# Tracing the last transposes of each half ahead of two block products in the MLP input of a decoder layer

## The chip, the cores and the metric

The kernel runs on one core of one Trainium2 chip. The metric is the device time of one execution in microseconds (us); the median of three runs of the kernel before is 2172.05 us (2169.45 to 2173.22).

## The reference

One decoder layer on a sequence of 2048 tokens of width 1024, in float32. The first part, a mixer of dilated attention and a gated recurrence, is not touched by the change. What matters here is the second part, the MLP, with its norms:

```python
def rms_norm(x, g):
    y = xf * lax.rsqrt(jnp.mean(xf * xf, axis=-1, keepdims=True) + NORM_EPS)
    return (y * g).astype(x.dtype)

def squared_relu_mlp(h, w1, w2):
    a = jax.nn.relu(h @ w1)
    return (a * a) @ w2

x = x + rms_norm(m, mix_norm_post[l])          # m: the mixer's output, (2048, 1024)
h = rms_norm(x, mlp_norm_pre[l])
x = x + rms_norm(squared_relu_mlp(h, w_ff_in[l], w_ff_out[l]), mlp_norm_post[l])
```

`w_ff_in` (w1) is 1024 x 4096, `w_ff_out` (w2) 4096 x 1024.

## The kernel before

**Precision.** Each float32 factor of a product is split in a high and a low part (`split`, L54): ScalarE (ACT) casts the high part (L56, rows named CAST), VectorE (DVE), in some places GpSimd (POOL), subtracts it to get the low part (L57). TensorE (PE) then does three matmuls per tile, high x high, low x high and high x low.

**Halves.** After the mixer's first part the kernel works through two halves of 1024 tokens (`half`, L2129, with hf = 0 and 1). Each half has eight blocks of 128 tokens, t = 0 to 7. For each block PE does the mixer's output projection (`OutProj.product`, L882, tiles m). `OutProj.finish` (L901) does the norm and residual on ACT and DVE; its last two DVE instructions (L927) write the normalised input h2 of the block into the tile xt, 512 columns each. xt's place is one of five in a ring of 128 x 1024 tiles, which also takes the loads of w1 (w1r).

**Columns.** `Factors.columns(t)` (L978) turns a block's h2 round: eight 128x128 transposes on PE (L989, tiles h2t), in two groups of four, q = 1 for the right half of xt and q = 0 for the left. ACT copies the first group out (L992); DVE, in the last four blocks, subtracts the second from it (L994) and so makes T3. Both tiles h2t come from a ring of two PSUM banks, B, which the tiles zc use as well. A block's transposes are traced two blocks after its norm; those of block 6 come after the first product of the MLP, those of block 7 later still.

**The MLP's input product** h @ w1 is done by a scheme of seven block products in place of eight (Strassen's in Winograd's form). The right factors are sums of blocks of h2, each with a high (hH) and a low (hL) part: B11, B21 and T3 are made in `columns`, T2, T4, T1 and B22 in `Factors.late` (L1009), after block 7's columns. Products 1 and 2 need B11 and B21, product 7 needs T3, product 6 T2, product 5 T1, product 3 B22, product 4 T4. Each needs all 512 columns of its factor. The left factors f are sums of blocks of w1; `mlp_in` (L1068) runs over 16 pairs j of rows of w1. For pairs 0 and 1, and for products 1 and 2 of pair 2 in the second half, they were made earlier and are loaded by SyncE (SP, L1094); the others are made from loads w1r (L1086) with sums on DVE (L1115). A pair is a generator whose steps are the products 1 (into PSUM tile za), 2 (zb), 7 (zc), 6, 5, 3 (again into za) and 4 (into zc); a product is 12 matmuls of 128x512 (L1104 to L1106). Between them ACT copies za to the tile sq (L1143 after product 1, L1148 after product 6, L1152 after 5), and only behind that copy may PE add the next product to za. Outputs are squared on ACT (L1109, L1110) and summed (L1113, L1167).

**What sets the order.** The code only traces instructions. A planner (`Plan`, L1496, with the simulation `Machine`, L1693) then gives each engine an order: it takes PE's instructions in about the order in which they were traced, as due times (`clock`), works back from them to the time at which each other instruction is needed (`need`), and simulates the engines, each taking the ready instruction that is needed first. An instruction on PE that isn't ready can be passed by a later one. The engines then keep to the order that comes out. So moving a step in the trace moves due times, and can move instructions on all engines.

The steps around the change, in `half`, with `pairs` the generators of the pairs:

```python
pairs = mlp_in(tc, sh, scr, hf, F.H, w1, w2, place)
next(pairs[0])                                   # pair 0: product 1
columns(NQH - 2)                                 # transposes of block 6
for j in (0, 1, 1, 2):                           # 0: product 2; 1: products 1, 2; 2: product 1
    next(pairs[j])
columns(NQH - 1)                                 # transposes of block 7
for j in (2, 0):                                 # 2: product 2; 0: product 7
    next(pairs[j])
```

Of the kernel before, what the change touches and what calls it, by code (L numbers as in the profile page):

```python
# [853 lines left out]
def mix_columns(nc, sh, scr, hf, order, t):  # L854

    mx = {}
    for g0 in range(0, KT, 4):
        n = f"{hf}_{t}_{g0}"
        hi, lo = sh.pair(f"m{n}", (P, 4, P))
        k0 = order[g0]  # L860
        sh.mixed = nc.sync.dma_start(out=f32(lo), in_=scr["mix"][hf][k0:k0 + 4, :, t * P:(t + 1) * P].rearrange("k p t -> p k t"))
        split_there(nc, hi, lo, nc.vector if hf and t == 0 else nc.gpsimd)
        for i, k in enumerate(order[g0:g0 + 4]):
            mx[k] = (hi[:, i, :], lo[:, i, :])
    return mx
# [321 lines left out]
def mlp_in_rest(pairs):  # L1187

    for j in range(0, NJ, 2):
        both = pairs[j:j + 2]  # L1190
        for i in TURNS[min(j // 2, 2)]:
            next(both[i])
        if j == NJ - 2:
            yield
        for x in both:
            next(x)
# [792 lines left out]
def trunk(tc, x, xT, g1, g2, g3, g4, w_in, w_v, conv_w, conv_b, w_r, b_r, w_i, b_i, lam, w_out, w1, w2,  # L1989
# [4 lines left out]
    def sb(name, side):  # L1994
        return tc.tile_pool(name=name, bufs=1, side=side, reuse_waits="tile")
# [5 lines left out]
    with (  # L2001
# [127 lines left out]
        def half(hf, wo, mx):  # L2129

            with contextlib.ExitStack() as st:
                F = Factors(nc, sh, hf, st.enter_context(sb(f"hA{hf}", "left")))
                h2 = {}
                po = st.enter_context(sb(f"op{hf}", "left"))
                with contextlib.nullcontext():

                    place = [po.tile([P, 4, TB], F32, name=f"place{hf}")]
                    op = OutProj(tc, sh, po, scr, hf, wo, order, x, g2, g3, sh.mixed if hf else None)

                    def columns(t):  # L2140
                        F.columns(cst["ident"], t, h2.pop(t))

                    for t in range(NQH):
                        m = [op.product(t, 0, mx[t])]
                        if t > 1:
                            columns(t - 2)
                        m.append(op.product(t, 1, mx[t]))
                        h2[t] = op.finish(t, m)
                        if t < NQH - 2:
                            with tc.issue_after(op.squared.ins):  # L2150
                                mx.append(mix_columns(nc, sh, scr, hf, order, t + 2))
                    wst.close()
                    F.tiles(st.enter_context(sb(f"hB{hf}", "right")), F.LATE)
                    pairs = mlp_in(tc, sh, scr, hf, F.H, w1, w2, place)
                    next(pairs[0])
                    columns(NQH - 2)
                    for j in (0, 1, 1, 2):
                        next(pairs[j])
                    columns(NQH - 1)
                    for j in (2, 0):  # L2160
                        next(pairs[j])
                    made = F.done
                    for step in (1, "T2", 0, "T4", 1, "T1", 0, 1, "B22"):
                        with tc.issue_after(made[0].ins), tc.issue_after(made[1].ins):
                            if step in F.LATE:
                                made = F.late(step)
                            else:
                                next(pairs[step])
                sh.made = made[1]
                end = mlp_in_rest(pairs)  # L2170
                next(end)
            return end
# [4 lines left out]

        with per, tc.manual_schedule(engines={mybir.EngineType.PE}):
            end = half(0, wo, ready)
            with sb("y0", "left") as pl, sb("z0", "left") as p:  # L2180
                rest = mlp_out(tc, sh, p, cst, scr, 0, w2, g4, out, pl)
# [19 lines left out]
                with tc.issue_after(cst["load"].ins):  # L2201
                    ready = [mix_columns(nc, sh, scr, 1, order, t) for t in range(2)]
            end = half(1, wo, ready)
            with sb("y1", "left") as pl, sb("z1", "left") as p:
                rest = mlp_out(tc, sh, p, cst, scr, 1, w2, g4, out, pl)
# [69 lines left out]
```

## Time and profile before

| | |
|---|---|
| median of three runs | 2172.05 us |
| the profiled execution's own time | 2171.24 us |
| its span, first to last instruction | 2169.4 us |
| mean granted clock of TensorE | 0.995 |
| busy: TensorE / VectorE / ScalarE / GpSimd | 98% / 70% / 58% / 22% |
| transposes of block 7, first and second half | at 707.66 and 1560.92 us |

The profile's rows name a line, an engine, an operation, the tile written, an arrow, the tiles read, their shapes and a count. In rows in order of time the first number is the start in us from the span's start, the second the duration; a bracket at the end tells how long the engine was idle just before, and what it waited for. Matmuls overlap: one starts about 0.23 us after the one ahead of it, and each lasts about 0.39. Rows of waits read "who <- for whom: us in total, times, longest". In the table by stretches the granted clock is given as a share of full speed, and the DMA share is the mean busy share of the core's 16 DMA engines.

### The profile page before, as it was taken

How to read it: one execution, taken by the hardware profiler on the slowest of the kernel's cores; microseconds unless marked ns; L12 is line 12 of the kernel's file. 1: busy time of each engine (PE TensorE's matmuls, PEld its weight loads, DVE VectorE, ACT ScalarE, POOL GpSimd, SP SyncE). 2: the span in 40 equal slices, each digit the busy share in tenths (PEclk: the TensorE clock that was granted, in tenths of full speed). 3: DMA queues.
4: the chain of work that ended last, by engine and by line, in shares of the span. 5: the costliest groups of instructions: out<-in, count | busy, mean ns of one | idle time of the engine just before them, and what ended most of it. 6: DMA issues, size and time to landing. Idle time of an engine off the chain costs nothing.

```text
span 2169.4 us, 30821 instructions
## 1 busy us (share of the span) xinstructions
PE 2129.0 (98%) x10232; PEld 1752.5 (81%) x10232; DVE 1510.2 (70%) x2883; ACT 1255.2 (58%) x2516; POOL 483.2 (22%) x552
## 2 busy tenths in 40 slices
PE   8999999999999999999999999999999999999998
PEld 6777878777788788888888888888788888888887
DVE  4468777768877777775776868787765665665556
ACT  6458666646554655554766667764465555654442
POOL 2454443477622001000011101113100000000003
PEclk9999999999999999999999999999999999999999
DMA  9555556456965667779787785796634444866665
GB/s 346 163 182 163 174 170 203 158 167 238 325 211 190 242 251 297 281 271 354 240 229 221 234 255 173 227 301 192 230 130 175 146 160 144 326 204 193 193 192 179
DMA packets 220899, 473.50 MB, mean 218 GB/s; under 512 B 23412, under 2 KB 74388, under 8 KB 214468
## 3 DMA queue, kind: packets, MB, share of 16 engines
q1 hardware_dynamic: 191924, 337.52, 48.2%
q0 software_dynamic: 28816, 134.01, 17.3%
q8 instruction: 81, 1.33, 0.3%
q14 instruction: 78, 0.64, 0.1%
HBM read 337.09 MB, written 151.13 MB: 225 GB/s over the span
## 4 chain that ended last, share of the span: by engine, by line
PE 84%; DVE 5%; ACT 5%; DMA 2%; POOL 2%; issue 2%; SPq 1%; DVEq 0%; ACTq 0%; POOLq 0%
PE o L1254 9%; PE o L1256 9%; PE o L1255 9%; PE za L1105 5%; PE za L1106 5%; PE za L1104 5%; PE z L229 4%; PE z L230 4%; PE z L231 4%; PE m L889 3%; PE m L891 3%; PE m L890 3%; PE zc L1105 3%; PE zc L1106 3%; PE zc L1104 3%; PE oB L672 2%
## 5 line engine op out<-in xcount | busy, mean ns | idle before, releaser
L229 PE MATMUL z<-hH,wH 128*128 128x512 f32 x576 | 228.8, 397 | 4.5 <-DVE zn L258 4.5
L231 PE MATMUL z<-hH,wL 128*128 128x512 f32 x576 | 228.4, 396 | 0.0
L230 PE MATMUL z<-hL,wH 128*128 128x512 f32 x576 | 228.2, 396 | 0.0
L229 PEld LDWEIGHTS z<-hH,wH 128*128 128x128 f32 x576 | 108.9, 189 | 31.1 <-DVE zn L258 5.8
L230 PEld LDWEIGHTS z<-hL,wH 128*128 128x128 f32 x576 | 108.9, 189 | 24.8 <-issue 4.5
L231 PEld LDWEIGHTS z<-hH,wL 128*128 128x128 f32 x576 | 108.8, 189 | 22.6 <-issue 2.3
L57 POOL TENSOR_TENSOR wL<-wraw,wH 128x512 fp32r<-128x512 f32 x68 | 100.6, 1491 | 101.9 <-ACT wH L56 80.8
L1169 POOL DMA_DIRECT2D sa<-sq x31 | 16.5, 532 | 375.2 <-ACT sq L1110 375.2
L1109 ACT ACTIVATE sq<-sq 128x512 f32<-128x512 f32 x93 | 58.8, 632 | 70.7 <-DVE sq L1113 70.7
L452 ACT ACTIVATE smB<-smB,stB 128x128 f32<-128x128 f32 (+3 forms) x128 | 71.5, 560 | 39.0 <-DVE stB L446 38.8
L452 ACT ACTIVATE sm<-sm,stA 128x256 f32<-128x256 f32 (+1 forms) x128 | 63.4, 497 | 50.9 <-DVE stA L446 50.7
L57 DVE TENSOR_TENSOR tlB<-pT_B,thB 128x384 fp32r<-128x384 f32 x96 | 57.2, 599 | 33.7 <-ACT thB L56 31.1
L1110 ACT ACTIVATE sq<-sq 128x512 f32<-128x512 f32 x124 | 76.9, 630 | 2.6
L446 DVE CUSTOM_DVE_ANT_0 sm<-S,mask_a 128x256 f32<-128x256 f32 (+1 forms) x128 | 47.7, 408 | 33.1 <-PE S L589 29.3
L1288 POOL TENSOR_TENSOR y<-y,g4b 128x512 f32<-128x512 f32 x8 | 12.5, 1578 | 257.1 <-ACT junk_y L86 257.1
L56 ACT CAST wH<-wraw 128x512 fp32r<-128x512 f32 x72 | 42.1, 616 | 43.5 <-PE z L230 24.5
L446 DVE CUSTOM_DVE_ANT_0 smB<-SB,mask_b 128x128 f32<-128x128 f32 (+3 forms) x128 | 59.6, 486 | 7.1 <-PE SB L647 3.6
L56 ACT CAST thB<-pT_B 128x384 fp32r<-128x384 f32 x96 | 48.9, 511 | 24.3 <-PE pT_B L425 19.6
L425 PE MATMUL pT_B<-ident,smB 128*128 128x128 f32 x320 | 59.6, 277 | 2.1 <-DVE tlA L57 1.2
L341 DVE SCALAR_TENSOR_TENSOR xc<-xr,cw,xc 128x512 f32<-128x512 f32 x48 | 48.1, 1001 | 6.7 <-POOL xc L338 6.4
L1104 PE MATMUL za<-hHT,f_6H 128*128 128x512 f32 x128 | 50.4, 395 | 1.7 <-ACT hHT L56 1.7
L1105 PE MATMUL za<-hLT,f_6H 128*128 128x512 f32 x128 | 50.7, 396 | 1.3 <-DVE hLT L57 1.3
(615 smaller groups left out, 7180.1 us busy)
## 6 DMA issues: line engine op xcount, KB each, us to landing
sa<-as POOLq DMA_DIRECT2D x31, 1024.0 KB, 6.9
w1r<-in_dram SPq DMA_DIRECT2D x56, 512.0 KB, 3.7
sa<-sq POOLq DMA_DIRECT2D x31, 768.0 KB, 3.9
wraw<-in_dram SPq DMA_DIRECT2D x72, 256.0 KB, 3.6
place<-in_dram SPq DMA_DIRECT2D x14, 1024.0 KB, 6.6
sb<-place POOLq DMA_DIRECT2D x14, 1024.0 KB, 4.3
vb<-sv SPq DMA_DIRECT2D x24, 512.0 KB, 6.1
kh<-sk SPq DMA_DIRECT2D x24, 512.0 KB, 5.5
```

The costliest lines, as they stand in the source:

```text
L57: (lo_eng or nc.vector).tensor_tensor(out=lo, in0=src, in1=f32(hi), op=ALU.subtract))
L229: pe.matmul(z, hi[:, k, :], hh, start=(k == 0), stop=False)
L230: pe.matmul(z, hi[:, k, :], hl, start=False, stop=False)
L231: pe.matmul(z, lo[:, k, :], hh, start=False, stop=(k == KT - 1))
L446: v.tensor_tensor_reduce(out=sm[:, c0:c0 + w], in0=sp[:, c0:c0 + w], in1=mask[:, mask.shape[-1] - w:], scale=1.0, scalar=3.0e38, op0=ALU.a ...
L452: s.activation(out=sm[:, c0:c0 + w], in_=sm[:, c0:c0 + w], func=AF.Exp, scale=-1.0, bias=st[:, 0, u, cols[j]:cols[j] + 1], accum_out=st[:, ...
L1104: pe.matmul(o, hi[:, k], bh[:, k], start=start and k == 0, stop=False, skip_group_check=True)
L1105: pe.matmul(o, hi[:, k], bl[:, k], start=False, stop=False, skip_group_check=True)
L1106: pe.matmul(o, lo[:, k], bh[:, k], start=False, stop=k == KH - 1, skip_group_check=True)
L1254: pe.matmul(o, ah[:, ts], bh, start=fresh and j == 0, stop=False, skip_group_check=True)
L1255: pe.matmul(o, ah[:, ts], bl, start=False, stop=False, skip_group_check=True)
L1256: pe.matmul(o, al[:, ts], bh, start=False, stop=j == NJ - 1, skip_group_check=True)
```

## The change

The transposes of block 7 are traced two steps earlier: after pair 0's product 2 and pair 1's product 1, and so ahead of pair 1's product 2 and pair 2's product 1. The order of the products among themselves is the same in the trace.

```diff
-                    next(pairs[0])
+                    for j in (0,):
+                        next(pairs[j])
                     columns(NQH - 2)
-                    for j in (0, 1, 1, 2):
+                    for j in (0, 1):
                         next(pairs[j])
                     columns(NQH - 1)
-                    for j in (2, 0):
+                    for j in (1, 2, 2, 0):
                         next(pairs[j])
```

On PE, in the first half, at the transposes of block 7. In the names hHB21 is the high part of B21, hLT1 the low part of T1; f0_1_2H is the high part of the left factor of half 0, pair 1, product 2; a last number tells tiles apart that are traced at different places.

```order
-L1106 MATMUL za0_2_7164<-hHB11_0_6248,f0_2_1L_7159 128x512
-L989 MATMUL h2t0_7_1_7177<-ident_60,xt7_6940 128x128 x4
-L989 MATMUL h2t0_7_0_7183<-ident_60,xt7_6940 128x128 x4
+L1104 MATMUL zb0_1_7157<-hHB21_0_6250,f0_1_2H_7153 128x512
+L1105 MATMUL zb0_1_7157<-hLB21_0_6251,f0_1_2H_7153 128x512
+L1106 MATMUL zb0_1_7157<-hHB21_0_6250,f0_1_2L_7154 128x512
+L1104 MATMUL zb0_1_7157<-hHB21_0_6250,f0_1_2H_7153 128x512
+L1105 MATMUL zb0_1_7157<-hLB21_0_6251,f0_1_2H_7153 128x512
+L989 MATMUL h2t0_7_1_7139<-ident_60,xt7_6940 128x128 x4
+L1106 MATMUL zb0_1_7157<-hHB21_0_6250,f0_1_2L_7154 128x512
+L989 MATMUL h2t0_7_0_7145<-ident_60,xt7_6940 128x128 x4
```

They stood behind the last matmul of pair 2's product 1. Now the first group stands behind the fifth matmul of pair 1's product 2, and the second one matmul later. In the second half all eight now stand behind the third matmul of that product.

On PE, in the first half, between the products 6 and 5 of the pairs 0 and 1:

```order
 L1106 MATMUL za0_0_7078<-hHT2_0_7066,f0_0_6L_7264 128x512
-L1104 MATMUL za0_0_7078<-hHT1_0_7070,f0_0_5H_7322 128x512
-L1105 MATMUL za0_0_7078<-hLT1_0_7071,f0_0_5H_7322 128x512
-L1106 MATMUL za0_0_7078<-hHT1_0_7070,f0_0_5L_7323 128x512
-L1104 MATMUL za0_0_7078<-hHT1_0_7070,f0_0_5H_7322 128x512
-L1105 MATMUL za0_0_7078<-hLT1_0_7071,f0_0_5H_7322 128x512
 L1104 MATMUL za0_1_7126<-hHT2_0_7066,f0_1_6H_7293 128x512
```

Five matmuls of pair 0's product 5 stood ahead of pair 1's product 6. Now they follow it, and product 5 is whole.

On DVE, in the second half, behind the subtraction that makes the last columns of T3 (L994). ws and w1r with 1_3 in their names are sums of pair 3's blocks of w1:

```order
-L994 TENSOR_TENSOR h2r1_12_14634<-h2r1_22_14637,h2t1_7_0_15573 128x4x128
-L1115 TENSOR_TENSOR ws1_1_3_15928<-w1r1_3_1_15881 128x512
-L1115 TENSOR_TENSOR w1r1_3_1_15881<-w1r1_3_0_15845,w1r1_3_1_15881 128x512
-L1115 TENSOR_TENSOR ws2_1_3_15929<-ws1_1_3_15928,w1r1_3_0_15845 128x512
+L994 TENSOR_TENSOR h2r1_12_14634<-h2r1_22_14637,h2t1_7_0_15537 128x4x128
 L57 TENSOR_TENSOR hLT3_1_14645<-h2r1_12_14634,hHT3_1_14644 128x4x128
```

The three sums of pair 3 stood directly behind that subtraction, ahead of T3's low part. Now the low part follows at once, and the sums stand six to seven instructions further back, among the splits of T4 and ahead of the last ones of T2. On ACT, in the first half, the copy of za of pair 1 (L1143) now follows all four casts of B22, where it stood behind three, and the copy L1148 of pair 0 follows it, where it stood ahead of the casts of B22. On SP, in the first half, the second load w1r of pair 3 now stands ahead of the loads of pair 1's factor 6, and a load w1r of pair 4 ahead of those of pair 0's factor 5; both stood behind. In the second half a load w1r of pair 4 now stands ahead of those of pair 1's factor 6. GpSimd's order differs by one swap of two stores. Behind pair 6 of the first half, and behind pair 3 of the second, the orders are the same.

## Prediction

> **What bounds the kernel now.** I read the page first, then the waits of TensorE (PE) at the two places that the change touches, then PE, VectorE (DVE) and ScalarE (ACT) there instruction by instruction. The page's head and its row of engines:
>
> ```profile
> span 2169.4 us, 30821 instructions
> PE 2129.0 (98%) x10232; PEld 1752.5 (81%) x10232; DVE 1510.2 (70%) x2883; ACT 1255.2 (58%) x2516; POOL 483.2 (22%) x552
> ```
>
> PE is busy for 98% of the span, so an edit pays only by what it takes from PE's 40 us of idle time, or from time in which PE runs slowly. Behind each of the two places PE has long stretches without a gap. Two rows of the table by stretches (length, then busy time of PE, PEld, DVE, ACT, POOL, then granted clock, DMA share, GB/s):
>
> ```profile
> 900.00:1000.00 100.00, 100.00 (x442) 82.64 (x442) 72.17 (x117) 56.69 (x101) 8.71 (x16) 1.00 0.80 298
> 2000.00:2100.00 100.00, 100.00 (x442) 82.78 (x442) 51.79 (x78) 46.62 (x77) 0.00 (x0) 1.00 0.62 195
> ```
>
> PE's waits between 660 and 760 us (first half), then between 1535 and 1645 us (second half), with total, times, longest:
>
> ```profile
> PE za L1104 <- ACT sq L1148: 1.0, 1, 1.0
> PE za L1105 <- DVE hLT L57: 0.8, 1, 0.8
> ```
>
> ```profile
> PE za L1104 <- ACT hHT L56: 1.7, 1, 1.7
> PE za L1105 <- DVE hLT L57: 1.3, 1, 1.3
> PE zc L1105 <- DVE hLT L57: 0.3, 1, 0.3
> ```
>
> All five are waits for the factors of the normalised input (hHT, hLT), or for a copy queued among their casts. PE at the first place (start, duration):
>
> ```profile
> 702.21 0.39 PE L1104 MATMUL zb<-hHB,f_2H 128*128 128x512 f32 x1
> ...
> 707.66 1.04 PE L989 MATMUL h2t<-ident,xt 128*128 128x128 f32 x8
> 708.45 0.48 PE L1104 MATMUL zb<-hHB,f_2H 128*128 128x512 f32 x1
> ...
> 711.27 0.61 PE L1104 MATMUL zc<-hHT,f_7H 128*128 128x512 f32 x2
> ...
> 716.71 0.39 PE L1104 MATMUL za<-hHT,f_6H 128*128 128x512 f32 x1
> ...
> 720.61 0.50 PE L1104 MATMUL za<-hHT,f_5H 128*128 128x512 f32 x1 [1.02 <-ACT sq L1148]
> 721.89 0.51 PE L1105 MATMUL za<-hLT,f_5H 128*128 128x512 f32 x1 [0.77 <-DVE hLT L57]
> ...
> 731.63 0.39 PE L1104 MATMUL za<-hHB,f_3H 128*128 128x512 f32 x1
> ```
>
> From 711.27 to 716.71 stand the two block products 7, 24 matmuls: 5.44 us, 0.227 us each, PE's undisturbed pace. From 716.71 to 731.63 stand the products 6 and 5 of two pairs, 48 matmuls. At the pace they take 10.88 us; they took 14.92. **The first half loses 4.04 us here**, part of it to the clock:
>
> ```profile
> 722.90:726.40 3.50, 3.50 (x10) 2.68 (x9) 3.50 (x7) 0.55 (x2) 0.00 (x0) 0.53 0.00 0
> 1570.60:1574.50 3.90, 0.91 (x3) 0.30 (x2) 3.90 (x8) 3.90 (x9) 0.00 (x0) 1.00 0.45 152
> ```
>
> Right behind the first half's wait PE ran 3.5 us at a granted clock of 0.53, which costs 3.5 x 0.47 = 1.6 us. During the second half's longer waits the clock stayed at 1.00. PE there:
>
> ```profile
> 1555.47 0.39 PE L1104 MATMUL zb<-hHB,f_2H 128*128 128x512 f32 x1
> ...
> 1560.92 1.04 PE L989 MATMUL h2t<-ident,xt 128*128 128x128 f32 x8
> ...
> 1564.53 0.61 PE L1104 MATMUL zc<-hHT,f_7H 128*128 128x512 f32 x2
> ...
> 1572.44 0.73 PE L1104 MATMUL za<-hHT,f_6H 128*128 128x512 f32 x2 [1.67 <-ACT hHT L56]
> 1574.52 0.50 PE L1105 MATMUL za<-hLT,f_6H 128*128 128x512 f32 x1 [1.35 <-DVE hLT L57]
> ...
> 1579.65 0.39 PE L1104 MATMUL za<-hHT,f_5H 128*128 128x512 f32 x1
> ```
>
> From 1564.53 to 1579.65 stand the products 7 and 6 of two pairs, again 48 matmuls: 15.12 us against 10.88. **The second half loses 4.24 us.**
>
> **The change, part by part.** Nothing is added or removed; in each half eight transposes (two groups of four) move up on PE. In the first half they now stand behind the fifth matmul of pair 1's product 2, with one matmul between the groups. The first group starts near 702.21 + 5 x 0.227 = 703.35, 4.3 us earlier; the second a group and a matmul later, near 704.1, 4.0 us earlier. In the second half all eight follow the third matmul: 1555.47 + 3 x 0.227 = 1556.15, 4.77 us earlier. Their own cost stays (707.66 to 708.45). The first matmul behind a group lasts 0.48 instead of 0.39, so the first half's extra break costs 0.09 us.
>
> Can they start there? They read xt, which DVE writes last. DVE, then ACT, in the first half:
>
> ```profile
> 702.17 1.41 DVE L927 SCALAR_TENSOR_TENSOR xt<-x,nm_x,g3b 128x512 f32<-128x512 f32 x2
> 708.91 0.69 DVE L994 TENSOR_TENSOR h2r<-h2r,h2t 128x512 f32<-128x512 f32 x1 [5.33 <-ACT h2r L992]
> 710.29 0.69 DVE L57 TENSOR_TENSOR hLT<-h2r,hHT 128x512 fp32r<-128x512 f32 x1 [0.69 <-ACT hHT L56]
> ...
> 712.10 2.51 DVE L57 TENSOR_TENSOR hLT<-h2r,hHT 128x512 fp32r<-128x512 f32 x4
> ...
> 719.34 2.49 DVE L57 TENSOR_TENSOR hLT<-h2r,hHT 128x512 fp32r<-128x512 f32 x4
> ```
>
> ```profile
> 719.98 0.58 ACT L1148 COPY sq<-za 128x512 f32<-128x512 f32 x1
> ...
> 722.02 0.59 ACT L1143 COPY sq<-za 128x512 f32<-128x512 f32 x1
> ```
>
> xt is whole at 702.17 + 1.41 = 703.58, 0.5 us ahead of the second group; the first needs only the first write, near 702.9. DVE then stood idle for 5.33 us: this is what the change uses. From 708.91 on its chain reaches T2 at 712.10 + 2.51 = 714.61 and T1 at 719.34 + 2.49 = 721.83. Moved up by 4.0 us, T2 is there near 710.6 and T1 near 717.8. PE gets to the products 6 at 716.7 and to the products 5 at 716.71 + 24 x 0.227 = 722.15, so neither waits. For in the new order pair 1's product 6 stands ahead of pair 0's product 5, and so the copy L1148 has 2.7 us of PE work as its cover; without it PE's 1.0 us wait would be back. Product 6 of pair 1 has to wait for L1143, which now follows four casts of B22. Before, a copy and three casts took from 719.98 to 722.02, 0.51 each; so L1143 starts at 719.98 - 4.0 + 4 x 0.51 = 718.0 and ends at 718.6, and PE needs it at 716.71 + 12 x 0.227 = 719.4. Only the 0.09 is left of the loss: **gain 3.95 us**.
>
> In this I count the slow stretch of 1.6 us as the wait's doing: it begins 1 us behind the wait's end, at 721.89, and no row shows one near it without a wait. The Trainium skill (TensorE: Matmul & The Clock Gate, "What's actually happening") halves the clock after an idle window of about 3.4 us, in windows that run freely. By that rule waits of 1.0 and 0.8 us don't halve it; the row at 0.53 speaks against that, or the stretch has another cause. By the rule 1.6 us of the gain would stay away, and the sum below would be 6.45 instead of 8.05 us. That is a rival below.
>
> xt's place is also freed earlier, and SyncE's queue (SP) puts the load of w1r that takes it ahead of pair 1's factor 6 (in the second half a later w1r load likewise). SP's issue of that factor, and the time to landing of the two factors 6:
>
> ```profile
> 704.89 0.32 SPq L1094 DMA_DIRECT2D f_6H<-sf  x1
> DMA to landing us min/median/max: 7.0/7.3/7.7
> ```
>
> The w1r load waits for the transposes until near 704.8 and holds up nothing else. The factor follows the end of product 2, now 0.8 us later, and lands by 704.89 + 0.8 + 7.7 = 713.4. The 512 KB ahead of it add, at the 298 GB/s quoted above, 1.8 us: 715.2, 4 us before its product. I take the queue at nothing.
>
> DVE in the second half:
>
> ```profile
> 1554.48 1.41 DVE L927 SCALAR_TENSOR_TENSOR xt<-x,nm_x,g3b 128x512 f32<-128x512 f32 x2
> ...
> 1562.18 0.69 DVE L994 TENSOR_TENSOR h2r<-h2r,h2t 128x512 f32<-128x512 f32 x1 [5.69 <-ACT h2r L992]
> 1562.78 0.68 DVE L1115 TENSOR_TENSOR ws<-w1r 128x512 f32<-128x512 f32 x1
> ...
> 1573.78 0.68 DVE L57 TENSOR_TENSOR hLT<-h2r,hHT 128x512 fp32r<-128x512 f32 x1
> ```
>
> xt is whole at 1555.89, 0.26 us ahead of the transposes. L994 moves to 1562.18 - 4.77 = 1557.41. The last of T2 followed it by 1573.78 + 0.68 - 1562.18 = 12.28 us, with three L1115 of pair 3 directly behind L994, about 1.8 us in all. These now come later, but still ahead of that last piece. In their old place 0.7 us of them lay in the time in which DVE waits for ACT's cast anyway (the 0.69 in brackets at 710.29); in the new place they lie in none. So the chain grows to about 12.9 us, and T2 is whole near 1570.35. The three L1115's shift is the one thing here that costs, and it is paid from the 4.77. PE asks for T2's low part behind 24 matmuls of the products 7 and two of the products 6: 1564.53 + 26 x 0.227 = 1570.4. There is no slack. The first L1115 will stand near 1562.4 and needs a load that was there by 1562.78, so a wait of 0 to 0.4 us may be left; I take 0.15, as nothing shows the load later than its need. The 0.3 at product 7 goes, since T3 no longer stands behind the L1115: **gain 4.1 us**.
>
> The sum is 3.95 + 4.1 = 8.05 us. The profiled execution took 2171.24 us (its span and 1.8 us around it) and would take 2163.2; it lies 0.8 under the median of 2172.05. **Forecast: 2172.05 - 8.05 = 2164.0 us**, -0.37%.
>
> **The rivals.** (1) *The slow clock isn't the wait's doing.* For it: the second half's 3.0 us of waits brought none (1.00 in the row from 1570.60), so the slow stretch may have a cause that stays. Then 2164.0 + 1.6 = 2165.6. Against it: its place, 1 us behind the wait's end. Chance 0.10.
>
> (2) *Half is given back.* In the attention between the halves the chain that ended last runs through loads as well:
>
> ```profile
> 1385.37 6.81 DMA b_12L<-sb
> ```
>
> If the first half's gain ends in such a wait, 2164.0 + 3.95 = 2168.0. Against it: these loads are issued as PE gives their tiles free, so they move with it. Chance 0.08. That both halves' gains are lost so, 2172: 0.06.
>
> (3) *Slower: the transposes wait for xt.* PE takes its instructions in order, so what was covered by 19 to 21 matmuls becomes a standstill if xt comes late. If it comes x us late in each half, PE stands for x in each, and the sum is 8.05 - 2x: up to x = 4.0 the change still gains, beyond that it costs. With x = 6.2 it is 2172.05 - 8.05 + 2 x 6.2 = 2176.4 us. The trace has xt ready 0.5 and 0.26 us ahead, and the order of DVE's work before xt is unchanged. Chance 0.06.
>
> **How the numbers follow.** The forecast has 0.70. About 0.2% (4.3 us) is what a measurement can tell from no change: faster is under 2167.7, slower over 2176.4. Faster: 0.70 + 0.10 and a little of (2), 0.82; same: 0.12; slower: 0.06. The best case has no rest of waits or breaks, 2163.8, and the runs of before lie from 2.6 us under their median to 1.2 over it; a half-clock stretch more or less in a median run is 1.6. Low: 2163.8 - 2.6 - 1.2 = 2160.0. High: case (2) with 1.0 for the runs, 2169.0.
>
> **What would show it.** Right: no PE wait on hHT, hLT or L1148 between 705 and 735, and at most 0.5 us in the second half's products 6; the 48 matmuls from the first product 6 to the first product 3 in about 10.9 us; the clock 1.00 there; L994 4 us earlier from the place's start. Wrong: a wait of the transposes, a wait on f_6 or L1143, a slow clock without a wait, or new PE waits further behind that add up to microseconds.

## The result and the profile after

| | before | changed |
|---|---|---|
| median of 8 runs each | 2169.64 us (2167.72 to 2173.22) | 2162.77 us (2159.86 to 2165.47) |
| the profiled execution's own time | 2171.24 us | 2162.82 us |
| its span | 2169.4 us | 2161.1 us |

The ratio is 0.9967, 95% interval 0.9958 to 0.9976: **6.9 us faster in the medians**, and 5.2 to 9.1 by the interval. Five more runs of the kernel before brought its median down from 2172.05 to 2169.64 us. The forecast was 2164.0 us. The head of the changed kernel's page and its row of engines:

```profile
span 2161.1 us, 30816 instructions
PE 2125.8 (98%) x10232; PEld 1749.5 (81%) x10232; DVE 1507.1 (70%) x2883; ACT 1256.7 (58%) x2516; POOL 484.3 (22%) x552
```

PE's busy time fell by 3.2 us and its idle time by 5.1 (40.4 to 35.3). Busy time can fall though no work went: matmuls at half the clock count as busy for about twice as long (eight transposes took 1.94 us at half the clock in a run below, and 1.04 at the full one). Not all of the 3.2 us is the change's: between 505 and 516 us, ahead of both places, the granted clock was 0.84 in the profile of before and 1.00 in this one.

PE's waits at the two places come first. In the first half (655 to 760 us) the view is empty. In the second (1530 to 1645 us) it has one row:

```profile
PE za L1105 <- DVE hLT L57: 1.0, 1, 1.0
```

Then the stretch from the first product 6 to the first product 3, 48 matmuls, in each half. The columns are length, busy time of PE, PEld, DVE, ACT, POOL, granted clock, DMA share, GB/s:

```profile
714.79:725.67 10.88, 10.88 (x49) 9.01 (x48) 10.85 (x19) 7.08 (x14) 0.00 (x0) 1.00 0.48 157
1564.73:1576.92 12.19, 11.17 (x49) 8.93 (x48) 9.49 (x16) 7.74 (x16) 0.00 (x0) 1.00 0.41 131
```

The first stretch is at PE's undisturbed pace, 10.88 us, at clock 1.00: nothing of the first half's loss is left. The second is 1.31 us over that pace; 1.02 of it is the wait itself. On PE (start, duration):

```profile
684.88 1.04 PE L989 MATMUL h2t<-ident,xt 128*128 128x128 f32 x8
...
701.41 0.60 PE L989 MATMUL h2t<-ident,xt 128*128 128x128 f32 x4
...
702.08 0.60 PE L989 MATMUL h2t<-ident,xt 128*128 128x128 f32 x4
...
725.67 0.39 PE L1104 MATMUL za<-hHB,f_3H 128*128 128x512 f32 x1
...
1564.73 0.61 PE L1104 MATMUL za<-hHT,f_6H 128*128 128x512 f32 x2
1566.36 0.50 PE L1105 MATMUL za<-hLT,f_6H 128*128 128x512 f32 x1 [1.02 <-DVE hLT L57]
```

Block 7's transposes start behind the fifth matmul of pair 1's product 2 without a wait. DVE, then ACT, in the first half:

```profile
702.79 0.69 DVE L994 TENSOR_TENSOR h2r<-h2r,h2t 128x512 f32<-128x512 f32 x1 [1.16 <-PE h2t L989]
...
713.22 2.49 DVE L57 TENSOR_TENSOR hLT<-h2r,hHT 128x512 fp32r<-128x512 f32 x4
```

```profile
715.94 0.58 ACT L1143 COPY sq<-za 128x512 f32<-128x512 f32 x1
717.71 0.58 ACT L1148 COPY sq<-za 128x512 f32<-128x512 f32 x1 [1.19 <-PE za L1106]
```

L994 waits for xt's transposes 1.16 us where it waited 5.33. T1 is whole at 715.71, and PE asks for it 24 matmuls behind 714.79, near 720.2. L1148, which PE waited for, now itself waits for PE. In the second half, SP's issues of w1r and DVE's work up to the end of T2's low part:

```profile
1551.41 1.08 SPq L1086 DMA_DIRECT2D w1r<-in_dram  x2
```

```profile
1558.35 0.69 DVE L1115 TENSOR_TENSOR ws<-w1r 128x512 f32<-128x512 f32 x1 [1.15 <-DMA w1r<-in_dram]
...
1565.62 0.68 DVE L57 TENSOR_TENSOR hLT<-h2r,hHT 128x512 fp32r<-128x512 f32 x1
```

T2's last piece ends at 1566.30, and PE goes on at 1566.36. DVE had stood 1.15 us for a load, at the first sum of pair 3, which stands ahead of that piece in DVE's order.

To compare kernels without the noise of the stages around, I cut each profiled execution at four rows: block 5's transposes and the first matmul of product 3, in each half (above: 684.88 and 725.67). The work between the two is the same in every kernel, whatever its order. "First" and "second" are these two places, "between" what lies between them, all in us:

| kernel | start | first | between | second | rest |
|---|---|---|---|---|---|
| before | 686.82 | 44.81 | 808.45 | 45.01 | 584.31 |
| before, second profile | 685.79 | 44.76 | 809.33 | 46.61 | 584.31 |
| changed | 684.88 | 40.79 | 809.13 | 42.12 | 584.18 |
| changed, second profile | 682.96 | 40.80 | 809.51 | 41.71 | 584.12 |
| changed, third profile | 682.19 | 40.80 | 808.91 | 40.90 | 584.10 |
| first half only | 684.57 | 40.80 | 809.18 | 46.41 | 584.34 |
| second half only | 681.48 | 44.73 | 809.76 | 41.05 | 584.08 |
| sums behind T2 | 682.12 | 40.80 | 809.62 | 40.79 | 584.17 |
| sums behind T2, second profile | 683.23 | 40.80 | 809.03 | 40.80 | 584.14 |
| next load later | 682.49 | 40.80 | 810.76 | 40.90 | 584.35 |
| T2 first | 684.70 | 40.80 | 809.79 | 40.77 | 584.14 |
| one product later | 684.82 | 41.46 | 810.77 | 44.50 | 584.35 |
| ahead of xt | 682.44 | 48.40 | 808.86 | 49.85 | 584.15 |

The rest agrees within 0.3 us in all thirteen. The start differs by 5.3 us although no kernel's order differs there, so a span alone says little. The two places are where the kernels differ.

### The profile page after: what moved, and what is told of

The parts are those of the page before. It is cut to its first block, busy times and chain, and to the rows that moved or that the text cites. A ratio compares the mean times of both kernels' runs of the same rounds, so it can differ in the third digit from the quotient of the medians.

```text
span 2161.1 us, 30816 instructions
## 1 busy us (share of the span) xinstructions
PE 2125.8 (98%) x10232; PEld 1749.5 (81%) x10232; DVE 1507.1 (70%) x2883; ACT 1256.7 (58%) x2516; POOL 484.3 (22%) x552
## 4 chain that ended last, share of the span: by engine, by line
PE 87%; ACT 4%; DVE 4%; DMA 2%; issue 2%; POOL 1%; SPq 0%; DVEq 0%; POOLq 0%; ACTq 0%
PE o L1254 9%; PE o L1256 9%; PE o L1255 9%; PE za L1105 5%; PE za L1106 5%; PE za L1104 5%; PE z L229 5%; PE z L230 5%; PE z L231 5%; PE zc L1106 3%; PE zc L1105 3%; PE zc L1104 3%; PE m L891 3%; PE m L889 3%; PE m L890 3%; PE oB L672 2%
## 5 line engine op out<-in xcount | busy, mean ns | idle before, releaser
L425 PEld LDWEIGHTS pT_B<-ident,smB 128*128 128x128 f32 x320 | 39.3, 140 | 14.7 <-DVE tlA L57 2.9
```

## The experiments

The theory: each half's gain is the PE waits that go there, the half-clock stretch behind them included, and what is missing in the second half is one new wait, at pair 3's first sum. The rivals are named in the expectations.

**The halves alone.** The number of steps ahead of block 7's transposes is set for each half (2 is the new order, 4 the old); the first kernel has the new order in the first half only, the second in the second:

```diff
-                    for j in (0, 1):
+                    cut = 4 if hf else 2          # second kernel: 2 if hf else 4
+                    for j in (0, 1, 1, 2, 2, 0)[:cut]:
                         next(pairs[j])
                     columns(NQH - 1)
-                    for j in (1, 2, 2, 0):
+                    for j in (0, 1, 1, 2, 2, 0)[cut:]:
                         next(pairs[j])
```

> Only the first half has the new order, the second the old one. Theory A (each half's gain is the PE waits that go there, the half-clock stretch included): 4.0 us under the kernel before, ratio 0.9982; in the trace the first half's 48 matmuls take 10.9 us at clock 1.00 and the second half's waits stand as before (products 7 and 6 of two pairs in 15.1 us). Rival B (the slow stretch of 1.6 us is not the waits' doing and comes and goes with something else): 2.4 us under, ratio 0.9989, on the average of its runs. Rival C (the gain comes from other places, since the changed kernel's profile is already 1.9 us ahead when it reaches the first place): under 1.5 us, with the rest absent from both halves alone.

Measured: 2167.04 us against 2168.77, ratio 0.9989 (0.9980 to 0.9997), so 0.7 to 4.3 us under, 1.7 in the medians. The interval holds theory A's 4.0 as well as rival B's 2.4: the time can't tell them apart. The places can. The first took 40.80 us where the old order took 44.81, 44.76 and 44.73. Rival C falls with that. The second half's waits stood as before, but behind them the clock now fell (rows of the table by stretches, wait and what follows it):

```profile
1565.10:1568.60 3.50, 0.84 (x3) 0.30 (x2) 3.50 (x7) 3.50 (x8) 0.00 (x0) 1.00 0.50 172
1568.60:1572.00 3.40, 3.01 (x7) 2.43 (x8) 3.40 (x7) 3.37 (x7) 0.00 (x0) 0.50 0.00 0
```

The same waits brought no such stretch in the first profile of the kernel before. So the second half, too, can lose 1.7 us to the clock, and its 15.1 us that were expected were not met: its place took 46.41 us, against 45.01 in that first profile.

> Only the second half has the new order. Theory A: 2.9 us under the kernel before (4.24 of waits go, 1.31 of a new one comes), ratio 0.9987; the two halves alone add up to the whole change's 6.9 us. In the trace the first half's waits (1.0 us on L1148, 0.8 us on hLT) are back, and behind them the clock falls again to about half for 3 to 4 us. Rival B: the waits are back, but the clock stays at 1.00 behind them. Rival C: well under 2.9 us.

Measured: 2164.48 us, ratio 0.9979 (0.9970 to 0.9988), 2.6 to 6.5 us under. The first half's waits of 1.0 and 0.8 us are back, and so is the slow clock behind them, as theory A said:

```profile
713.90:717.40 3.50, 1.70 (x7) 0.92 (x6) 3.50 (x7) 3.50 (x8) 0.00 (x0) 1.00 0.54 173
717.40:720.80 3.40, 3.40 (x10) 2.68 (x9) 3.40 (x7) 0.45 (x2) 0.00 (x0) 0.52 0.00 0
```

Not expected: the view shows no wait of PE in the second half. Its place took 41.05 us where the changed kernel's first profile, with the same order there, took 42.12.

**The rest wait in the second half.** In the first of two edits of the changed kernel the planner may issue pair 3's first sum, and so the two that follow it, only behind the second matmul of pair 0's product 6, which needs all of T2. In the second, SP may issue the load of pair 4 only behind pair 1's factor 5:

```diff
-            sub(S1, a21, a22, ALU.add)
+            sub(S1, a21, a22, ALU.add); hf and j == 3 and tc.behind.append((nc.cur_bb.bb.instructions[-1].name, scr["T2"]))
...
-        product(a, 6, False)
+        product(a, 6, False); j or scr.update(T2=nc.cur_bb.bb.instructions[-11].name)
```

```diff
-            nc.sync.dma_start(out=t, in_=w1[2 * j + f])
+            with tc.issue_after(scr[1, 5].ins) if hf and (j, f) == (4, 0) else contextlib.nullcontext(): nc.sync.dma_start(out=t, in_=w1[2 * j + f])
...
-                    nc.sync.dma_start(out=t, in_=d)
+                    scr[j, m] = nc.sync.dma_start(out=t, in_=d)
```

> The changed kernel, but in the second half VectorE's three sums L1115 of pair 3 stand behind the last piece of T2 instead of ahead of it. Theory A (the rest wait in the second half comes from the first of these sums, which waits 1.15 us for its w1r load and holds up what is queued behind it): no PE wait in the products 6, the 48 matmuls in 10.9 instead of 12.2 us, 1.0 to 1.3 us under the changed kernel, so 7.9 to 8.2 us under the kernel before, ratio 0.9963. Rival D (T2 is late for another reason, ScalarE's casts or GpSimd's sums): the wait of about 1 us stays and the time is the changed kernel's. Rival E (the sums are late for pair 3 now): a new wait at pair 3's product 7, and no gain.

Measured: 2159.46 us, ratio 0.9958 (0.9946 to 0.9971). No PE wait, second place 40.79 us, no new wait behind it. T2's last piece and the first sum on DVE, and the first matmul on PE that reads T2's low part:

```profile
1560.33 0.68 DVE L57 TENSOR_TENSOR hLT<-h2r,hHT 128x512 fp32r<-128x512 f32 x1
...
1563.33 0.68 DVE L1115 TENSOR_TENSOR ws<-w1r 128x512 f32<-128x512 f32 x1
```

```profile
1562.68 0.39 PE L1105 MATMUL za<-hLT,f_6H 128*128 128x512 f32 x1
```

T2 is whole at 1561.01, 1.7 us ahead of that matmul, and no sum that needs a load stands ahead of it on DVE any more. Rivals D and E fall by the trace. The changed kernel was not timed beside this one here.

> The changed kernel, but in the second half SyncE issues the load of pair 4's first w1r behind pair 1's factor 5 instead of directly behind pair 3's second w1r. No other engine's order changes. Theory A1 (the load that the sum waits for is late because the next load of 512 KB shares the DMA engines with it): the load lands 1 us sooner after its issue, VectorE's wait of 1.15 us falls under 0.3 and PE's wait of 1.0 us under 0.3; 0.8 to 1.0 us under the changed kernel. Theory A2 (it is late because it is issued late, and the factors' loads around it fill the engines anyway): both waits stay within 0.3 us of what they were, and the time is the changed kernel's.

Measured: 2161.07 us, ratio 0.9963 (0.9951 to 0.9976); the interval overlaps the changed kernel's, so the time doesn't decide. The loads of w1r that SP issues here, and then the times from issue to landing (min, median, max) of the loads between 1540 and 1565 us, first in the changed kernel's profile and then in this one:

```profile
1550.78 0.33 SPq L1086 DMA_DIRECT2D w1r<-in_dram  x1
...
1559.36 0.42 SPq L1086 DMA_DIRECT2D w1r<-in_dram  x1
```

```profile
DMA to landing us min/median/max: 5.0/6.2/7.4
```

```profile
DMA to landing us min/median/max: 4.9/5.0/5.1
```

These views need care: of the three loads in each, the trace has no landing for the one that the sum waits for, pair 3's second. The other two are pair 3's first, issued 6.5 us ahead of its second, and pair 4's; the middle number is only their mean. Pair 4's load took 7.4 us where it went out 0.75 us behind the other, and 4.9 here.

On DVE and on PE in the kernel with the next load later:

```profile
1556.38 0.69 DVE L1115 TENSOR_TENSOR ws<-w1r 128x512 f32<-128x512 f32 x1
...
1563.65 0.68 DVE L57 TENSOR_TENSOR hLT<-h2r,hHT 128x512 fp32r<-128x512 f32 x1
```

```profile
1564.44 0.44 PE L1105 MATMUL za<-hLT,f_6H 128*128 128x512 f32 x1
```

The sum starts 5.60 us after the issue of its load (1550.78) without a wait, so the load was there by then; in the changed kernel it started 6.94 us after it (1551.41 to 1558.35), with a wait. T2 is whole at 1564.33, and PE reads it at 1564.44 without a wait. From the start of the first sum to T2's end it is 7.95 us here and 7.95 in the changed kernel (1558.35 to 1566.30). So DVE's wait of 1.15 us passes on in full, and without it nothing is to spare.

This is what theory A1 foretold, but in one profile, and the order with both loads back to back went without a PE wait in two of its four profiles (second half only, and the changed kernel's third below). So A1 is not shown. What speaks for it is pair 4's load: it took 6.1 to 7.4 us in the six profiles in which it went out 0.75 us behind pair 3's at this place, and 4.7 to 4.9 in the four in which it went out 4.8 us or more behind (this one, both of the kernel before, and first half only).

**The changed kernel again.** It was run and profiled twice more, unaltered.

> The changed kernel once more, unaltered, for a second look and to be timed beside the others. Theory A (the rest wait hangs on a load whose time to landing differs between executions; 6.2 and 7.4 us for the two loads in the changed kernel's first profile, 5.8 and 6.6 in the kernel with the second half alone, whose order there is the same): PE's wait in the second half's products 6 is anywhere from 0 to 1.0 us, and on the average of its runs the kernel is 6 to 7.5 us under the kernel before, ratio 0.9965 to 0.9972. Rival (the wait belongs to the order): it is 1.0 us again.

> The changed kernel a third time, beside the other two. Theory A: the first place 40.8 us again; in the second PE waits 0 to 1.0 us, as the load of pair 3's second w1r lands 5.8 to 7.4 us after its issue; no stretch at half the clock in either place, since no stop of PE there exceeds 1.0 us.

Measured: 2161.90 us, ratio 0.9961 (0.9949 to 0.9974), and 2161.25 us, ratio 0.9962 (0.9949 to 0.9974). The first ratio's centre is a little under what was expected. (The 6.2 and 5.8 us in the first expectation are means of the kind just told, not times of the load that the sum waits for, and the times of that load in the second expectation rest on them.) SP's issue of the two loads and the sum's row, second profile first:

```profile
1549.89 1.08 SPq L1086 DMA_DIRECT2D w1r<-in_dram  x2
```

```profile
1556.41 0.69 DVE L1115 TENSOR_TENSOR ws<-w1r 128x512 f32<-128x512 f32 x1 [0.73 <-DMA w1r<-in_dram]
```

```profile
1548.58 1.08 SPq L1086 DMA_DIRECT2D w1r<-in_dram  x2
```

```profile
1554.23 0.69 DVE L1115 TENSOR_TENSOR ws<-w1r 128x512 f32<-128x512 f32 x1
```

From the issue of its load to the sum's start it was 6.94, 6.52 and 5.65 us in the three profiles; the sum waited 1.15, 0.73 and 0 us for the load, and PE's rest wait was 1.0, 0.6 and 0 us. So the wait goes with the load, whose time differs between executions of one and the same order. In neither profile did the clock fall at either place.

> The kernel with the three sums of pair 3 behind T2 once more, to be timed beside the changed kernel. Theory A: no PE wait in either place, each place 40.8 us from the transposes of the 128 tokens before the last to the first product 3, 0.9 us under the changed kernel's second place on the average of its two profiles (42.12 and 41.71); 0.5 to 2 us under the changed kernel in the medians. Rival E: a wait elsewhere takes it back, and the medians agree.

Measured: 2160.90 us, ratio 0.9961 (0.9947 to 0.9975), 0.35 under the changed kernel beside it. (The expectation names the place's first row wrongly; it is block 5's transposes, as in the table.) Both places took 40.80 us. Over all runs the kernel with the sums behind T2 has a mean of 2160.7 us (10 runs, standard deviation 2.5) and the changed kernel 2162.3 (18 runs, 1.8). It never waits in the trace; whether it is faster, these runs don't settle.

**A shorter lead.** Block 7's transposes stand one product ahead of their old place in place of two (`cut = 3` in both halves).

> The transposes of each half's last 128 tokens stand behind pair 1's product 2, one product ahead of their old place, 1.6 us (first half) and 2.0 us (second half) later than in the changed kernel. Theory A (T2 and T1 have time to spare in the first half and none in the second): in the first half no PE wait; in the second half T2's low part comes about 2 us later than in the changed kernel and PE waits 0.7 to 2 us for it in the products 6; the time lies 0.5 to 2.5 us over the changed kernel's, the more where a half-clock stretch follows the wait. Rival F (the last steps of the lead bring nothing): no wait in either half and the changed kernel's time.

Measured: 2163.66 us, 1.8 over the changed kernel beside it, ratio 0.9970 (0.9957 to 0.9983). PE's one wait in the second half is of the size expected, and a slow stretch followed:

```profile
1569.38 0.50 PE L1105 MATMUL za<-hLT,f_6H 128*128 128x512 f32 x1 [1.82 <-DVE hLT L57]
```

```profile
1569.90:1573.40 3.50, 3.50 (x10) 2.69 (x10) 3.50 (x7) 2.52 (x5) 0.00 (x0) 0.53 0.02 5
```

The second place took 44.50 us, so in this profile half of the lead kept only 1.5 of the 5.2 us between 46.0 and 40.8. But the profiled execution, 2167.66 us, is the slowest of the six that were timed, 4.0 over their median, so the place may cost less in the others. The first half had a wait, which I had not expected: 0.4 us on L1143, the copy that the prediction had found to be queued behind the casts of B22.

**T2 first.** An edit of the changed kernel that gates pair 3's first sum behind T2's third piece (DVE to DVE) and so makes that piece urgent:

```diff
-            made = self.split(b, {"T2": t2, "T4": t4, "T1": t2, "B22": b22}[b], cs)
+            made = self.H[b, c] = self.split(b, {"T2": t2, "T4": t4, "T1": t2, "B22": b22}[b], cs)
...
-            sub(S1, a21, a22, ALU.add)
+            with tc.issue_after(H["T2", 2][1].ins) if hf and j == 3 else contextlib.nullcontext(): sub(S1, a21, a22, ALU.add)
```

> The changed kernel, with the third piece of T2 in the second half made urgent for the planner (pair 3's first sum may be issued only behind it), so that VectorE and ScalarE make T2's pieces ahead of T4's; the transposes stand three matmuls later there. Theory A: T2 is whole well before PE asks for it, no PE wait in the products 6, the time that of the kernel with the sums behind T2, 1.0 to 2.0 us under the changed kernel. Rival G (T4 or the copies L1143, which now stand behind T2's casts, become late instead): a new wait at products 6 to 4 and no gain.

Measured: 2161.37 us, ratio 0.9957 (0.9945 to 0.9970). No wait, second place 40.77 us, as theory A said; but only 0.5 us under the changed kernel beside it, less than expected and less than these runs can tell.

**The kernel before, again.**

> The kernel before once more, unaltered, one look. Theory H (a stop of PE of 1.8 to 3 us brings a stretch of about 3.45 us at half the clock in some executions and not in others; so far behind the first half's waits in two of two profiles and behind the second half's in one of two): the waits stand as before, 1.8 us in the first half and 3.3 in the second; each may or may not have the slow stretch behind it, and where it has, it is 3.4 to 3.5 us long at 0.50. Rival B (the slow stretch comes at places of its own): a stretch in one of the two halves without a wait within 2 us ahead of it.

Measured: 2172.60 us. All five waits stood as in the first profile, and this time each half had its slow stretch:

```profile
721.70:725.20 3.50, 3.50 (x10) 2.71 (x9) 3.50 (x7) 0.55 (x2) 0.00 (x0) 0.51 0.00 0
1575.00:1578.50 3.50, 3.50 (x10) 2.71 (x9) 3.50 (x7) 2.51 (x5) 0.00 (x0) 0.52 0.02 5
```

**Too early.** Behind the planner's work, block 7's transposes are taken out of PE's order and put in front of pair 0's product 2, directly behind block 6's:

```diff
+def ahead(q, acc):
+    out = lambda k: next(x[6] for x in acc[k] if x[5])
+    for hf in range(2):
+        moved = [k for k in q if out(k).startswith(f"h2t{hf}_{NQH - 1}_")]
+        for k in moved:
+            q.remove(k)
+        at = next(x for x, k in enumerate(q) if out(k).startswith(f"zb{hf}_0_"))
+        q[at:at] = moved
```

> The changed kernel with the transposes of the last 128 tokens put on TensorE directly behind those of the 128 tokens before them, 29 (first half) and 27 matmuls (second half) earlier still; the other engines' orders are the changed kernel's. This is the prediction's rival 3 with x made large. Theory A: TensorE stands for xt, 6.2 us in the first half and 5.3 in the second (from the first write of xt in the changed kernel's profile to the place where the transposes would start), and nothing makes it good; with a slow stretch of 1.7 us behind none, one or both, the kernel is 10.5 to 14 us over the changed kernel and 3 to 7 over the kernel before, ratio 1.0014 to 1.0032. Rival I (the delay of what follows the stop is made good by the waits that it covers further behind): within 3 us of the changed kernel.

Measured: 2178.03 us against 2170.91, ratio 1.0031 (1.0019 to 1.0042): slower than before, and 16.8 us over the changed kernel. The transposes in each half:

```profile
698.63 1.94 PE L989 MATMUL h2t<-ident,xt 128*128 128x128 f32 x8 [6.09 <-issue]
...
1555.60 1.94 PE L989 MATMUL h2t<-ident,xt 128*128 128x128 f32 x8 [5.80 <-ACT hHT L56]
```

The stops, 6.1 and 5.8 us, are near what was worked out (6.2 and 5.3). Over the kernel before it is 7.1 us in the medians, at the top of what was expected; over the changed kernel it is more than the 10.5 to 14, and the places say why: 48.40 and 49.85 us are 7.6 and 9.05 over 40.80, so 1.5 and 3.25 us came behind the stops. The eight transposes took 1.94 us in place of 1.04: PE set out at half the clock.

```profile
694.60:701.40 6.80, 2.77 (x11) 2.61 (x12) 5.28 (x13) 1.08 (x4) 0.00 (x0) 0.50 0.94 324
1554.70:1561.60 6.90, 6.00 (x18) 5.08 (x19) 4.67 (x9) 3.62 (x8) 0.00 (x0) 0.51 0.08 33
```

These stretches are 6.8 us long, twice the usual, and they begin during the stops. PE was busy for 2.77 and 6.00 us of them, which at half the clock costs about 1.4 and 3.0 us, near the 1.5 and 3.25; the expectation had counted at most 1.7 for each. Rival I falls: nothing was made good.

## Why the prediction was right, and where it was not

**The first half** went as told. Forecast 3.95 us, measured 44.77 - 40.80 = 3.97 us (means of three profiles of the old order and eight of the new; the shorter lead and the transposes ahead of xt are left out). Transposes without a wait, L1148 hidden, L1143 in time.

**The slow clock** was counted as the waits' doing, and it was (rival 1 falls). The old order had it in the first half in three profiles of three, the new one in none of eight. By the Trainium skill (TensorE: Matmul & The Clock Gate, "What's actually happening") the clock is halved after an idle window of about 3.4 us. Here waits of 1.8 us within 2.3 us were enough, in three profiles of three, so the window needn't be idle throughout.

**The second half** came out near the forecast by two errors that offset each other. Forecast 4.1 us; measured 46.01 - 41.45 = 4.56 us (means of three old and four new profiles).

- The step "during the second half's longer waits the clock stayed at 1.00" took one execution for the rule. In two profiles of three the stretch was there, 1.7 us each: on the average 1.0 us more to gain than the 4.24 counted (46.01 against 45.01).
- The step "a wait of 0 to 0.4 us may be left; I take 0.15, as nothing shows the load later than its need" was mis-sized: PE's wait was 1.0, 0.6, 0 us in the changed kernel and 0 in the kernel with the second half alone. It rests on "I take the queue at nothing", which was worked out for the first half only. In the kernel before SP issued the two loads in question 4.8 us apart:

```profile
1557.17 0.33 SPq L1086 DMA_DIRECT2D w1r<-in_dram  x1
...
1561.99 0.33 SPq L1086 DMA_DIRECT2D w1r<-in_dram  x1
```

  The earlier transposes free xt's place, and so both loads go out back to back. That the second makes the first late is likely and not shown (see the next load issued later, above). The prediction saw that a later w1r load is put forward "likewise" and did not ask what it would travel beside. Its chain was right: from L994 to T2's end it forecast 12.9 us, and where the load wasn't late, in the third profile, it took 12.95 (1549.23 to 1562.18). "There is no slack" was right to 0.1 us, and so the whole delay reached PE.

**Given back between the halves** (rival 2): between the places it took 809.18 us on the average behind the old order (three profiles) and 809.49 behind the new (eight), with ranges of 1.3 and 1.9 us. A loss of 0.3 us is possible and not shown; half the gain was not lost.

**Slower for want of xt** (rival 3): the mechanism is real and its price formula, 8.05 - 2x, was too kind. With x = 5.95 us on the average it gives 3.9 us slower; the run was 6.7 us slower by its ratio (4.1 to 9.1), since PE also sets out at half the clock behind such a stop.

**The sum.** 8.05 us was forecast. The places give 3.97 + 4.56 = 8.5; the times give 6.9 us in the first comparison, 8.5 and 8.2 by the ratios of the two later ones, and 7.4 over all runs taken together (50 of before, median 2169.65; 18 of the changed kernel, 2162.27). With single runs 2 us apart these agree. That the forecast of 2164.0 us came within 1.2 of the measured 2162.77 is in part luck: its base, the median of three runs, lay 2.4 us over that of 8, and its gain lay 1.2 over the 6.9 of that comparison. The low end of the range takes off a last 1.2 us for which the prediction gives no source.

## What to carry to other kernels

When an edit starts a step earlier, follow the places that it frees: a load that is let in earlier may travel beside another and make it late, and whoever waits for the late one pays, with all that is queued behind it on its engine. A short stop of PE costs more than its length, so price it with a chance of the slow stretch behind it, and take that chance from several profiles. Where whole runs scatter by 2 us, cut each profile at two rows around the edit and compare the pieces.

## What the runs showed of the hardware

At the two places a stretch at half the clock follows a stop of PE, of nearly the same length each time: 3.4 to 3.5 us at 0.50 to 0.53; with the stops of 6 us it was twice as long and began during the stop. Counted over both places of the thirteen profiles, stops of 1.8 us or more (waits that lie within 4 us taken together) had it 8 times of 9; stops of 1.0 us or less never (3); and at the 14 places without a stop there was none. Whether a stop of 3.0 us brings it differs between executions of the same kernel: the second half's waits in the kernel before had none in one profile and one in the next.

The 8 of 9 doesn't carry over to the rest of the kernel. Near 505 us, long ahead of both places, PE stands for 1.6 to 3.0 us in every profile, for a matrix product that the change doesn't touch, and only in 5 of the 13 does the clock fall there. PE's wait and the clock there, first in the first profile of before and then in the kernel with T2 first:

```profile
511.17 0.56 PE L229 MATMUL z<-hH,wH 128*128 128x512 f32 x1 [2.97 <-DVE zn L258]
```

```profile
505.00:516.00 11.00, 8.03 (x28) 4.93 (x27) 11.00 (x11) 9.18 (x14) 10.80 (x11) 0.84 0.62 193
```

```profile
509.73 0.49 PE L229 MATMUL z<-hH,wH 128*128 128x512 f32 x1 [3.00 <-DVE zn L258]
```

```profile
505.00:516.00 11.00, 8.00 (x34) 5.56 (x33) 11.00 (x11) 7.73 (x12) 10.80 (x11) 1.00 0.61 177
```

So the length of a stop alone doesn't decide; what else does stays open. By the Trainium skill (TensorE: Matmul & The Clock Gate, "What's actually happening") the clock is set by windows of about 3.4 us that run freely; the length of the stretches and the differences between executions agree with that.
